# Seven block products for eight in the right half of the feed-forward down projection of a two-layer decoder trunk

## The chip, the cores and the metric

The kernel runs on one core of a Trainium2 chip. The metric is the device time of one execution in microseconds; less is better. Five engines work side by side, each through its own queue of instructions: TensorE (PE in the profile, with its weight loads as PEld), VectorE (DVE), ScalarE (ACT), GpSimd (POOL) and SyncE (SP), which here only issues DMAs. Matmul results go to PSUM, eight banks of 128 x 512 float32; everything else lives in SBUF.

## The reference

Batch 1, 256 tokens, model width 1024, two layers. Layer 0 has a dilated sliding-window attention, layer 1 a forgetting attention; each is followed by a feed-forward block with 2816 hidden features. What the change touches is the second product of that block:

```python
def swiglu(h, w_gu, w_down):
    gu = h @ w_gu
    g, u = gu[..., :D_FF], gu[..., D_FF:]
    return (jax.nn.silu(g) * u) @ w_down

def reference(x, ...):
    h = x
    for i in range(DEPTH):
        ...                                   # h = h + mixer(rmsnorm(h, ...), ...)
        h = h + swiglu(rmsnorm(h, ffn_norm[i]), ffn_w_gu[i], ffn_w_down[i])
    return rmsnorm(h, final_norm)
```

All of it is float32.

## The kernel before

**Products.** Every projection runs on TensorE in the type float32r. To keep float32 precision each operand is split into a high part (the value rounded to float32r) and a low part (what is left), and a product is three matmuls: high x high, high x low, low x high (`mm3`, L200 to L211). `mm3(o, stat, mov, ...)` loads the stationary operand, 128 columns of it, and streams the moving operand; with `narrow` the second and third matmul are cut into two halves of the columns.

**Weights.** They come in pieces of 128 x 2048 float32, two DMAs of 512 KB each into the tile `raw` (five buffers). `split` (L76) makes the high part on ScalarE (L80, `wh<-raw`) and the low part on VectorE (L84, `wl<-raw,wh`). `order` lists all pieces in the order of their use; `weights(nm, i)` returns a piece and on the way prepares the next ones, up to two ahead in the program's text. `wh` and `wl` have four buffers each.

**Order of instructions.** The kernel is written on a framework that traces it and then orders each engine's queue itself, by priority (the place in the program) and by what is ready in its own model of the time; it also draws all semaphores and gives tiles their buffers in turn. `first()` raises the priority of what stands under it by 300 instructions, `tc.issue_after` keeps an instruction behind another one.

**The feed-forward block** (`ffn`, L702, once per layer). The hidden features come in 22 blocks of 128. `up(f)` computes block f for all 256 tokens: `proj_feat` makes g, 8 products of 256 columns each (24 matmuls), ScalarE takes Silu of it (L728), a second `proj_feat` makes u, VectorE multiplies the two (L730), and `split` makes the high and low part of the result (`ah`, `al`). g goes to a PSUM bank with the tag `mm`, u to one with the tag `tr`; each tag has two banks. The first three blocks are computed token-wise and transposed instead.

Two blocks make one down piece j (11 of them per layer, NJ = 11; LATE = 8). `down(j, t)` adds, for the token half t (128 tokens), the product of the activations (stationary, 128 hidden features x 128 tokens) with the weights (moving, 512 columns) into two PSUM banks, the left 512 and the right 512 columns of the output: `acc[0]` in the banks `sc`, `acc[1]` in the banks `o`. With two halves of tokens, two blocks of hidden features and two halves of columns that is 8 products of 512 columns, 24 matmuls per piece. The sums stay in these four banks over all 11 pieces. So all eight banks are in use: `mm` and `tr` for the up projections, `sc` and `o` for the sums. Pieces alternate: after every even block f from 4 on, piece f/2 - 1 is added (piece 0 after block 3). The last pieces are taken out of order, so that the two token halves end at different times and the next stage can begin on the first; the last one in layer 1 puts its right half in two products of 256 columns in banks of their own.

Of the kernel before, what the change touches and what calls it, by code (L numbers as in the profile page):

```python
# [10 lines left out]
F32 = mybir.dt.float32  # L11
# [6 lines left out]
P = 128  # L18
# [14 lines left out]
def trunk(ctx: ExitStack, tc: tile.TileContext, T, out):  # L33
# [10 lines left out]
    def first():  # L44

        return tc.high_priority(offset=300)

    def psum(tag):
        return ps.tile([P, 512], F32, tag=tag, name=f"ps_{tag}", bufs=2)
# [26 lines left out]
    def split(pair, view, src, early=True, after=None, hold=None):  # L76
        hi, lo = pair
        with first() if early else nullcontext():
            with behind_(hold):
                a = nc.scalar.activation(view(hi), src, AF.Copy)  # L80

            def low(after=None):
                with tc.issue_after(after.ins) if after else nullcontext():
                    return nc.vector.tensor_tensor(view(lo), src, view(hi).bitcast(F32), op=ALU.subtract)  # L84

            if isinstance(after, list):
                return after.append(low)
            return a, low(after)


    def piece(key, todo=None):
        if key[0][:2] == "dn" and key[1] == LATE:
            wh, wl = (y.rearrange("p k c -> p (k c)") for y in fm_tile("ot", KT, 1))
        else:
            wh, wl = (wp.tile([P, WIDE], F32R, tag=y, name=y, bufs=4) for y in ("wh", "wl"))
        if key == GATED:
            wh, wl = (y.rearrange("p (k c) -> p k c", k=KT) for y in (wh, wl))
        for c in range(2):
            raw = wp.tile([P, 1024], F32, tag="raw", name="raw", bufs=5)
            u = slice(c * 1024, (c + 1) * 1024)  # L100
            nc.sync.dma_start(raw, T[key[0]][key[1]][:, u])
            view = lambda y, u=u: y[:, u]
            if key == GATED:
                raw = raw.rearrange("p (k c) -> p k c", c=256)
                view = lambda y, c=c: y[:, c * 4:c * 4 + 4, :256]
            cut = lambda after=None, hold=None, raw=raw, view=view: split((wh, wl), view, raw, False, after, hold)
            if todo is None:
                cut()
            else:
                todo.append(cut)  # L110
        if key == GATED:
            cut = lambda after=None, hold=None: split((wh, wl), lambda y: y[:, :, 256:], wf32, False, after, hold)
            todo.append(cut)
        return wh, wl

    def fm_tile(tag, n, bufs):
        return tuple(ap.tile([P, n, S], F32R, tag=f"{tag}{x}", name=f"{tag}{x}", bufs=bufs) for x in "hl")
# [31 lines left out]
        order += [(f"dn{l}", NJ - 1)]  # L149
    AHEAD = 2  # L150
    ready = {}
    state = {"next": 0}

    def weights(nm, i, after=None, ahead=AHEAD, hold=None):
# [56 lines left out]
    def both(pair, *idx):  # L211
        return tuple(x[idx] for x in pair)
# [84 lines left out]
    def transposed(blocks, copy=nc.vector.tensor_copy, tag="tr", home="pt"):  # L297

        tr = psum(tag)
        for i, b in enumerate(blocks):  # L300
            nc.tensor.transpose(tr[:, i * P:(i + 1) * P], b, ident)  # L301
        n = len(blocks) * P
        bufs, cols = {"pt": (3, 640), "bias": (4, 6 * P)}[home]
        w = ap.tile([P, cols], F32, tag=home, name="pt", bufs=bufs)
        with first():
            copied["last"] = copy(w[:, :n], tr[:, :n])
        return w
# [64 lines left out]
    def plus(a, b):  # L372
        return nc.vector.tensor_tensor(a, a, b, op=ALU.add)
# [328 lines left out]
    def ffn(l, hs, xt, grow, mid):  # L702
        acc = {}
        acts = {}

        def act(f):
            if f % 2 == 0:
                acts[f // 2] = tuple(p_tile(512, F32R, f"a{y}") for y in "hl")
            return acts[f // 2], lambda y: y[:, (f % 2) * S:(f % 2 + 1) * S]

        def gated(g, u, shape):
            sa = ap.tile([P, 512], F32, tag="qr", name="sa", bufs=3)
            sg, a = (sa[:, i * S:(i + 1) * S].rearrange("p (a b) -> p a b", a=shape) for i in range(2))
            nc.scalar.activation(sg, g, AF.Silu)
            nc.vector.tensor_tensor(a, u, sg, op=ALU.mult)
            return a

        def up(f):
            wt = weights(f"gu{l}", f)
            with first() if f == NF - 1 else nullcontext():  # L720
                up_with(f, wt)

        def up_with(f, wt):
            sa = ap.tile([P, 512], F32, tag="qr", name="sa", bufs=3)
            sg, a = (sa[:, i * S:(i + 1) * S] for i in range(2))
            g, u = (psum(tag)[:, :S] for tag in ("mm", "tr"))
            proj_feat(xt, wt, g, 0)
            nc.scalar.activation(sg, g, AF.Silu)  # L728
            proj_feat(xt, wt, u, 1)
            nc.vector.tensor_tensor(a, u, sg, op=ALU.mult)  # L730
            split(*act(f), a)

        def down(j, t, by_f=None, narrow=False):

            wt = dn[j]
            if j == 0:
                acc[t] = [psum(("sc", "o")[t]) for _ in range(2)]
            cols = [(0, 512, acc[t][0][:, :512]), (512, 512, acc[t][1][:, :512])]
            own = l == 1 and t == 1 and j == NJ - 1
            if own:  # L740

                acc[t][1:] = psum("mm"), psum("tr")
                cols[1:] = (512, 256, acc[t][1][:, :256]), (768, 256, acc[t][2][:, :256])
            nf = [(c, f) for c in cols for f in range(2)]
            if by_f is not None:
                nf = [(c, f) for f in by_f for c in cols]
            for (a, b, o), f in nf:
                i = mm3(o, both(acts[j], ALL, slice(f * S + t * P, f * S + (t + 1) * P)),
                        both(wt, ALL, slice(f * D + a, f * D + a + b)), f == 0 and (j == 0 or own and a >= 512),
                        f == 1 and (j == NJ - 1 or l * t * a > 0 and j == NJ - 2), narrow and (a, b, f) == (512, 512, 1))  # L750
            return i


        dn = {}
        ws = [weights(f"gu{l}", f) for f in range(2)]
        pair = [psum(("o", "mm")[l]) for _ in range(2)]
        rows = {}

        def gate(t):
            gu = pair[t].rearrange("p (a c b) -> p a c b", a=2, c=2)  # L760
            rows[t] = gated(gu[:, :, 0, :], gu[:, :, 1, :], 2)

        for half in range(2):
            proj_pair(xt, ws[half], pair, half, (0,))
        gate(0)
        wt, o = weights(f"gu{l}", 2), psum(("mm", "o")[l])
        proj_tok(xt, wt, o[:, :S], 0, hook=(2, lambda: norm_t(*hs[1], grow, xt, 1)))
        for half in range(2):
            proj_pair(xt, ws[half], pair, half, (1,))
        gate(1)  # L770
        proj_tok(xt, wt, o[:, S:], 1)
        tr = psum("tr")
        for f in range(2):
            for t in range(2):
                nc.tensor.transpose(tr[:, f * S + t * P:f * S + (t + 1) * P], rows[t][:, f, :], ident)
        act(0)
        split(acts[0], lambda y: y, tr)
        third = act(2)
        up(3)
        gu = o.rearrange("p (a c b) -> p a c b", a=2, c=2)  # L780
        a = gated(gu[:, :, 0, :], gu[:, :, 1, :], 2)
        tr = psum("tr")
        for t in range(2):
            nc.tensor.transpose(tr[:, t * P:(t + 1) * P], a[:, t, :], ident)
        split(*third, tr[:, :S])
        for f in range(2, NF):
            if f > 3:
                up(f)
            if f % 2 == 0:
                j = f // 2 - 1  # L790
                dn[j] = weights(f"dn{l}", j)
                down(j, 0, narrow=j >= LATE)
                if j < LATE:
                    down(j, 1, narrow=True)
        dn[NJ - 1] = weights(f"dn{l}", NJ - 1)
        down(LATE, 1)
        last = down(NJ - 1, 0, (0, 1))
        res = [residual(acc[0], hs[0][0], f"hf{l}0")]
        with tc.issue_after(last.ins):
            down(NJ - 2, 1)  # L800
            if l == 0:
                down(NJ - 1, 1, (0,))
            else:
                h1 = hs[1][0][:, 512:]
                with first():
                    nc.vector.tensor_tensor(h1, acc[1][1], h1, op=ALU.add)
            mid(res[0])
            down(NJ - 1, 1, (1,) if l == 0 else None)
        res.append(residual(acc[1], hs[1][0], f"hf{l}1") if l == 0 else (acc[1], hs[1][0]))
        return res  # L810
# [328 lines left out]
```

## Time and profile before

| | |
|---|---|
| median of 3 runs | 735.55 us (734.79 to 736.73) |
| the profiled execution | 736.1 us |
| its span, first to last instruction | 734.3 us |
| mean granted TensorE clock | 0.997 |
| busy: PE, PEld | 726.4 us (99%), 672.4 us (92%) |
| busy: DVE, ACT, POOL | 495.9 us (68%), 388.7 us (53%), 83.0 us (11%) |
| DMA | 141.93 MB, mean 193 GB/s |

A row of the page or of a view names line, engine and operation, then what is written and read (`out<-in`, tile names of the program without buffer numbers), the shapes, and how many. Behind a bar stand busy time and mean duration, behind a second bar the idle time of the engine just before these instructions and what ended it. In the timeline a row begins with the start in microseconds and the duration; the idle time before it stands in square brackets. TensorE's matmuls are pipelined, so their durations overlap and the distance between starts tells the pace. In a table of windows, each engine has its busy time in that stretch and in brackets the number of its instructions.

The two feed-forward blocks run from about 253 to 436 us and from about 545 us to the end. One period of their middle part, two up projections and one down piece, takes 16.4 us.

### The profile page before, as it was taken

Reading aid. Unit: us, or ns where it says so; the run is one execution under the profiler, and the core shown is the slowest. Engines: PE = TensorE matmul, PEld = TensorE weight load, DVE = VectorE, ACT = ScalarE, POOL = GpSimd, SP = SyncE. Lnnn points to the kernel's source line nnn. Section 1 sums busy time; section 2 is a strip of 40 time slices with the busy share of each in tenths; the row PEclk is TensorE's granted clock in tenths of the full one; section 3 lists DMA queues with packets and bytes.
Section 4 is the critical chain, followed back from the end, with each engine's and each line's share of the span. In section 5 each row is a group of like instructions: output and inputs, shape, how many; then the busy total and the mean of one; then the engine's idle time right before and its main releaser. Section 6 shows DMA issues by size and latency. Waiting matters only on the chain.

```text
span 734.3 us, 14310 instructions
## 1 busy us (share of the span) xinstructions
PE 726.4 (99%) x5856; PEld 672.4 (92%) x5856; DVE 495.9 (68%) x762; ACT 388.7 (53%) x617; POOL 83.0 (11%) x118
## 2 busy tenths in 40 slices
PE   9999999999999999999999999999999999999996
PEld 7999989999988899999999989999889999999995
DVE  6997998998996775554555474576776554556533
ACT  7646747738445663444554453587475444545421
POOL 0600206007105000000000004110010000000001
PEclk9999999999999999999999999999999999999998
DMA  9865955956864376656567352874547656656601
GB/s 335 306 202 174 237 182 153 289 193 152 268 194 160 116 241 221 195 179 203 195 202 247 127 168 90 294 260 138 172 142 237 222 179 203 195 188 218 198 1 58
DMA packets 55042, 141.93 MB, mean 193 GB/s; under 512 B 20257, under 2 KB 21441, under 8 KB 54977
## 3 DMA queue, kind: packets, MB, share of 16 engines
q1 hardware_dynamic: 54832, 140.88, 59.4%
q8 instruction: 46, 0.75, 0.4%
q14 instruction: 20, 0.16, 0.1%
q10 hardware_dynamic: 144, 0.15, 0.1%
HBM read 136.00 MB, written 1.07 MB: 187 GB/s over the span
## 4 chain that ended last, share of the span: by engine, by line
PE 97%; DVE 1%; ACT 1%; POOL 0%; issue 0%; POOLq 0%; DVEq 0%; ACTq 0%
PE ps_mm L208 34%; PE ps_mm L203 17%; PE ps_tr L208 9%; PE ps_sc L208 8%; PE ps_o L208 7%; PE ps_tr L203 5%; PE ps_sc L203 4%; PE ps_o L203 4%; PE ps_o L313 2%; PE ps_sc L395 2%; PE ps_tr L196 1%; PE ps_tr L301 1%; PE ps_sc L476 1%; PE ps_o L322 1%; PE ps_sc L894 0%; PE ps_sc L458 0%
## 5 line engine op out<-in xcount | busy, mean ns | idle before, releaser
L80 ACT ACTIVATE wh<-raw 128x1024 fp32r<-128x1024 f32 x236 | 243.4, 1054 | 207.1 <-PE ps_tr L208 66.7
L84 DVE TENSOR_TENSOR wl<-raw,wh 128x1024 fp32r<-128x1024 f32 x236 | 288.3, 1242 | 82.6 <-ACT wh L80 82.4
L203 PE MATMUL ps_mm<-xt,wh 128*128 128x256 f32 x816 | 227.2, 279 | 0.2 <-ACT v L281 0.2
L208 PE MATMUL ps_mm<-xt,wl 128*128 128x256 f32 x816 | 226.0, 277 | 0.0
L208 PE MATMUL ps_mm<-xt,wh 128*128 128x256 f32 x816 | 226.0, 277 | 0.0
L203 PEld LDWEIGHTS ps_mm<-xt,wh 128*128 128x128 f32 x816 | 153.1, 188 | 2.2 <-issue 1.7
L208 PEld LDWEIGHTS ps_mm<-xt,wl 128*128 128x128 f32 x816 | 153.6, 188 | 0.1
L208 PEld LDWEIGHTS ps_mm<-xt,wh 128*128 128x128 f32 x816 | 153.4, 188 | 0.0
L208 PE MATMUL ps_tr<-xt,wh 128*128 128x256 f32 x304 | 83.9, 276 | 0.0
L208 PE MATMUL ps_tr<-xt,wl 128*128 128x256 f32 x304 | 83.9, 276 | 0.0
L203 PE MATMUL ps_tr<-xt,wh 128*128 128x256 f32 x304 | 83.7, 276 | 0.0
L730 DVE TENSOR_TENSOR sa<-ps_tr,sa 128x256 f32<-128x256 f32 x38 | 16.1, 424 | 73.5 <-PE ps_tr L208 73.5
L208 PEld LDWEIGHTS ps_tr<-xt,wh 128*128 128x128 f32 x304 | 57.1, 188 | 0.0
L208 PEld LDWEIGHTS ps_tr<-xt,wl 128*128 128x128 f32 x304 | 57.0, 188 | 0.0
L203 PEld LDWEIGHTS ps_tr<-xt,wh 128*128 128x128 f32 x304 | 57.0, 188 | 0.0
L203 PE MATMUL ps_mm<-wh,xt 128*128 128x512 f32 (+1 forms) x144 | 49.8, 346 | 0.0
L173 POOL TENSOR_SCALAR rs<-ssq 128x1 f32<-128x1 f32 x7 | 1.9, 271 | 420.6 <-ACT junk L182 420.6
L208 PE MATMUL ps_mm<-wl,xt 128*128 128x512 f32 (+1 forms) x149 | 49.1, 335 | 0.0
L208 PE MATMUL ps_mm<-wh,xt 128*128 128x512 f32 (+1 forms) x149 | 49.1, 335 | 0.0
L285 POOL COPY v<-v 32x256 f32<-32x256 f32 x64 | 40.5, 632 | 71.2 <-ACT v L281 68.6
L203 PE MATMUL ps_sc<-wh,ah 128*128 128x512 f32 x80 | 31.4, 392 | 0.0
L208 PE MATMUL ps_sc<-wl,ah 128*128 128x512 f32 (+1 forms) x82 | 31.3, 385 | 0.0
(232 smaller groups left out, 1113.6 us busy)
## 6 DMA issues: line engine op xcount, KB each, us to landing
raw<-in_gu SPq DMA_DIRECT2D x88, 512.0 KB, 4.8
raw<-in_a_in SPq DMA_DIRECT2D x68, 512.0 KB, 5.0
raw<-in_dn SPq DMA_DIRECT2D x44, 512.0 KB, 4.7
raw<-in_b_in SPq DMA_DIRECT2D x24, 512.0 KB, 5.0
raw<-in_a_out SPq DMA_DIRECT2D x8, 512.0 KB, 5.0
raw<-in_b_out SPq DMA_DIRECT2D x8, 512.0 KB, 4.4
bias<-sums SPq DMA_DIRECT2D x8, 384.0 KB, 6.6
grow<-in_norms SPq DMA_DIRECT2D x4, 512.0 KB, 5.7
```

Source lines behind the costliest of these rows:

```text
L80: a = nc.scalar.activation(view(hi), src, AF.Copy)
L84: return nc.vector.tensor_tensor(view(lo), src, view(hi).bitcast(F32), op=ALU.subtract)
L196: nc.tensor.transpose(tr[:, k * P:(k + 1) * P], xn[:, kk * P:(kk + 1) * P], ident)
L203: nc.tensor.matmul(o, sh, mh, start=start, stop=False)
L208: last = nc.tensor.matmul(o[:, u], s, m[:, u], start=False, stop=end and u.stop == n)
L285: nc.gpsimd.tensor_copy(v[1 + a % 2][n:n + 32, a // 2 * S:a // 2 * S + S], by_t[a * 32:a * 32 + 32, t, g])
L301: nc.tensor.transpose(tr[:, i * P:(i + 1) * P], b, ident)
L313: nc.tensor.matmul(o[h * HD:(h + 1) * HD], v[:, c:c + HD], w(h), start=start, stop=stop)
L322: nc.tensor.matmul(o[:, :n], mhalf.to_broadcast([P, P]), mhalf.to_broadcast([P, n]), start=True, stop=True)
L395: nc.tensor.matmul(lead[t], xt[y][:, k, t * P:(t + 1) * P], w[z][:, u], start=k + y + z == 0, stop=k == KT - 1 and z == 1)
L476: nc.tensor.matmul(sc[h][c, o:o + 64], q[HR[h], pr, qb * P + a * 32:qb * P + a * 32 + 32], k[HR[h], pr].rearrange("p (b n) -> p b n", b=2) ...
L730: nc.vector.tensor_tensor(a, u, sg, op=ALU.mult)
```

## The change

In pieces 0 to 7 of each layer, the right half of the output is computed by Strassen's scheme in Winograd's form. For one piece the right half is a product of two 2 x 2 matrices of blocks: two token halves x two blocks of hidden features, times two blocks of hidden features x two column groups of 256. Eight block products become seven, with sums of blocks made beforehand on both sides and sums of products afterwards.

- `sums_of` takes the place of the loop in `piece` for these weights. From the four 128 x 256 blocks it makes four sums on VectorE; one overwrites a block of `raw`, three go to a tile of 768 columns (`ts`, tag `pt`) that is split like a weight (`th`, `tl`, tag `bias`).
- `combine` makes four sums of activation blocks with three instructions on VectorE (`sa4`, tag `pt`) and splits them (`sh`, `sl`, tag `v`). For this the unsplit activations of a pair of blocks are kept together (`pair_of`, tag `qr`); for the first three blocks ScalarE copies them from PSUM.
- `down` computes only the left columns in these pieces, without `narrow`; `down_7` adds the seven products of 256 columns into seven areas of 256 columns: three in the right banks of `acc`, four in two more banks, `acc["x"]`.
- `acc["x"]` takes the two `tr` banks from piece 0 to piece 7. So in every `up` after the first blocks, g and u share one bank with the tag `mm`, g in columns 0 to 255, u in columns 256 to 511.
- `gather`, after piece 7, adds the products that belong to several output blocks to the residual rows h (a copy on ScalarE, eight additions on VectorE) and so frees the `tr` banks.
- The first product of the right half that follows for the second token half (piece 8) is done in two groups of 256 columns, as half of that bank has not been written before.

```diff
@@ piece
+        if key[0][:2] == "dn" and key[1] < LATE:
+            todo += sums_of(key, (wh, wl))
+            return wh, wl
         for c in range(2):
...
+    def sums_of(key, w):
+
+        raw = [wp.tile([P, 1024], F32, tag="raw", name="raw", bufs=5) for _ in range(2)]
+        for c in range(2):
+            nc.sync.dma_start(raw[c], T[key[0]][key[1]][:, c * 1024:(c + 1) * 1024])
+        b11, b12, b21, b22 = (raw[f][:, c:c + S] for f in range(2) for c in (512, 768))
+        sums = ap.tile([P, 768], F32, tag="pt", name="ts", bufs=3)
+        t3, t2, t4 = (sums[:, i * S:(i + 1) * S] for i in range(3))
+        pair = tuple(ap.tile([P, 768], F32R, tag="bias", name=f"t{y}", bufs=4) for y in "hl")
+        summed[key] = pair
+
+        def plus(o, a, b):
+            nc.vector.tensor_tensor(o, a, b, op=ALU.add)
+
+        def cut(c, after=None, hold=None):
+            if c == 0:
+                plus(t3, b12, b22)
+                plus(b12, b11, b12)
+            elif c == 2:
+                plus(t2, b22, b12)
+                plus(t4, t2, b21)
+                return split(pair, lambda y: y, sums, False, after, hold)
+            return split(w, lambda y: y[:, c * 1024:(c + 1) * 1024], raw[c], False, after, hold)
+
+        return [lambda after=None, hold=None, c=c: cut(c, after, hold) for c in range(3)]
@@ ffn
+        rows_f = {}
+        combos = {}
+
+        def pair_of(j):
+            if j not in rows_f:
+                rows_f[j] = ap.tile([P, 512], F32, tag="qr", name="a2", bufs=3)
+            return rows_f[j]
+
+        def combine(j, a):
+
+            y = ap.tile([P, 512], F32, tag="pt", name="sa4", bufs=3)
+            b = a.rearrange("p (b c) -> p b c", c=P)
+            z = y.rearrange("p (b c) -> p b c", c=P)
+            with first():
+                nc.vector.tensor_tensor(z[:, :2], b[:, 1:2].to_broadcast([P, 2, P]), b[:, 0:4:3], op=ALU.subtract)
+                nc.vector.tensor_tensor(z[:, 2], z[:, 1], b[:, 0], op=ALU.subtract)
+                nc.vector.tensor_tensor(z[:, 3], b[:, 2], z[:, 2], op=ALU.add)
+            combos[j] = tuple(ap.tile([P, 512], F32R, tag="v", name=f"s{x}", bufs=7) for x in "hl")
+            split(combos[j], lambda y: y, y)
+
+        def down_7(j):
+
+            if j == 0:
+                acc["x"] = [psum("tr") for _ in range(2)]
+            c11, c12, c21, _, p1, p6, q5, q7 = (x[:, i * S:(i + 1) * S]
+                                                for x in (acc[0][1], acc[1][1], *acc["x"]) for i in range(2))
+            a, w, s, t = acts[j], dn[j], combos[j], summed[f"dn{l}", j]
+            for o, (st, i), (mv, c) in ((p1, (a, 0), (w, 512)), (c11, (a, 2), (w, D + 512)), (c12, (s, 3), (w, D + 768)),
+                                        (c21, (a, 3), (t, 512)), (q5, (s, 1), (w, 768)), (p6, (s, 2), (t, S)),
+                                        (q7, (s, 0), (t, 0))):
+                mm3(o, both(st, ALL, slice(i * P, (i + 1) * P)), both(mv, ALL, slice(c, c + S)),
+                    j == 0 and any(o is y for y in (p1, c11, c21, q5)), j == LATE - 1 and any(o is y for y in (p6, q7)))
+
+        def gather():
+
+            (p1, p6), (q5, q7) = ((x[:, :S], x[:, S:]) for x in acc["x"])
+            y = ap.tile([P, 512], F32, tag="pt", name="u", bufs=3)
+            u, d = y[:, :S], y[:, S:]
+            h0, h1 = hs[0][0], hs[1][0]
+            c0, c1 = slice(512, 768), slice(768, 1024)
+            nc.scalar.activation(d, p1, AF.Copy)
+            for o, x, z, op in ((u, d, p6, ALU.add), (h0[:, c0], h0[:, c0], d, ALU.add), (d, q5, u, ALU.subtract),
...
@@ up_with
-            sa = ap.tile([P, 512], F32, tag="qr", name="sa", bufs=3)
-            sg, a = (sa[:, i * S:(i + 1) * S] for i in range(2))
-            g, u = (psum(tag)[:, :S] for tag in ("mm", "tr"))
+            sg = ap.tile([P, 512], F32, tag="qr", name="sa", bufs=3)[:, :S]
+            a = pair_of(f // 2)[:, f % 2 * S:(f % 2 + 1) * S]
+            o = psum("mm")
+            g, u = o[:, :S], o[:, S:]
             proj_feat(xt, wt, g, 0)
             nc.scalar.activation(sg, g, AF.Silu)
             proj_feat(xt, wt, u, 1)
             nc.vector.tensor_tensor(a, u, sg, op=ALU.mult)
             split(*act(f), a)
+            if f % 2 and 1 < f // 2 < LATE:
+                combine(f // 2, rows_f.pop(f // 2))
@@ down
-            cols = [(0, 512, acc[t][0][:, :512]), (512, 512, acc[t][1][:, :512])]
+            cols = [(0, 512, acc[t][0][:, :512])]
+            if j >= LATE:
+                cols.append((512, 512, acc[t][1][:, :512]))
...
+                if (j, t, a, f) == (LATE, 1, 512, 0):
+
+                    st = both(acts[j], ALL, slice(P, 2 * P))
+                    for c in (0, S):
+                        mm3(o[:, c:c + S], st, both(wt, ALL, slice(a + c, a + c + S)), False, False)
+                    continue
@@ the loop of ffn
                 down(j, 0, narrow=j >= LATE)
                 if j < LATE:
-                    down(j, 1, narrow=True)
+                    down(j, 1)
+                    down_7(j)
+                if j == LATE - 1:
+                    gather()
```

The tag `pt` grows from 640 to 768 columns. For the first three blocks the same activations are also copied (`pair_of(0)`, `rows_f[1]`) and combined.

More of the change, by code (lines that the diff above doesn't have):

```diff
@@ L151, in trunk @@
     ready = {}
+    summed = {}
     state = {"next": 0}
@@ L302, in transposed @@
         n = len(blocks) * P
-        bufs, cols = {"pt": (3, 640), "bias": (4, 6 * P)}[home]
+        bufs, cols = {"pt": (3, 768), "bias": (4, 6 * P)}[home]
         w = ap.tile([P, cols], F32, tag=home, name="pt", bufs=bufs)
@@ new lines, in gather @@
+        def gather():
[6 more added lines that the diff above has]
+            for o, x, z, op in ((u, d, p6, ALU.add), (h0[:, c0], h0[:, c0], d, ALU.add), (d, q5, u, ALU.subtract),
+                                (h0[:, c1], h0[:, c1], d, ALU.add), (h1[:, c1], h1[:, c1], d, ALU.add),
+                                (h1[:, c1], q7, h1[:, c1], ALU.add), (h1[:, c0], h1[:, c0], u, ALU.add),
+                                (h1[:, c0], h1[:, c0], q7, ALU.subtract)):
+                nc.vector.tensor_tensor(o, x, z, op=op)
@@ L777, in ffn @@
         split(acts[0], lambda y: y, tr)
+        nc.scalar.activation(pair_of(0), tr, AF.Copy)
+        combine(0, rows_f.pop(0))
         third = act(2)
@@ L785, in ffn @@
         split(*third, tr[:, :S])
+        nc.scalar.activation(rows_f[1][:, :S], tr[:, :S], AF.Copy)
+        combine(1, rows_f.pop(1))
         for f in range(2, NF):
```

## The prediction

> **What bounds the kernel now.** I read the page first: engines, then the chain that ended last, then who waited for whom.
>
> ```profile
> span 734.3 us, 14310 instructions
> PE 726.4 (99%) x5856; PEld 672.4 (92%) x5856; DVE 495.9 (68%) x762; ACT 388.7 (53%) x617; POOL 83.0 (11%) x118
> ...
> PE 97%; DVE 1%; ACT 1%; POOL 0%; issue 0%; POOLq 0%; DVEq 0%; ACTq 0%
> ```
>
> TensorE (PE) is the chain. The list of PE's own waits has two lines for the whole kernel:
>
> ```profile
> PE ps_o L322 <- DVE mhalf L66: 0.9, 1, 0.9
> PE ps_mm L203 <- ACT v L281: 0.2, 1, 0.2
> ```
>
> So time is won only by giving PE fewer columns to stream, and lost as soon as PE has to wait. What a column costs is read from start to start in the timeline of PE (the durations overlap). One down piece, and the ends of the up projection (one feature block) around it:
>
> ```profile
> 299.19 0.28 PE L203 MATMUL ps_mm<-xt,wh 128*128 128x256 f32 x1
> ...
> 301.80 0.28 PE L208 MATMUL ps_mm<-xt,wl 128*128 128x256 f32 x1
> 301.91 0.28 PE L203 MATMUL ps_tr<-xt,wh 128*128 128x256 f32 x1
> ...
> 304.63 0.39 PE L203 MATMUL ps_sc<-wh,ah 128*128 128x512 f32 x1
> 304.87 0.40 PE L208 MATMUL ps_sc<-wl,ah 128*128 128x512 f32 x1
> 305.10 0.39 PE L208 MATMUL ps_sc<-wh,al 128*128 128x512 f32 x1
> 305.33 0.39 PE L203 MATMUL ps_sc<-wh,ah 128*128 128x512 f32 x1
> 305.56 0.39 PE L208 MATMUL ps_sc<-wl,ah 128*128 128x512 f32 x1
> ...
> 307.37 0.39 PE L203 MATMUL ps_o<-wh,ah 128*128 128x512 f32 x1
> ...
> 309.64 0.40 PE L208 MATMUL ps_o<-wl,ah 128*128 128x256 f32 x2
> 309.87 0.40 PE L208 MATMUL ps_o<-wh,al 128*128 128x256 f32 x2
> 310.11 0.29 PE L203 MATMUL ps_mm<-xt,wh 128*128 128x256 f32 x1
> 310.23 0.28 PE L208 MATMUL ps_mm<-xt,wh 128*128 128x256 f32 x1
> ```
>
> An up projection is 48 matmuls of 256 columns, 299.19 to 304.63: 0.1133 us each. The piece lasts 310.11 - 304.63 = 5.48 us. It has 24 products of 512 columns; the last two are cut into 2 x 256. In steady state a 512 takes 0.227 us (307.37 to 309.64 is 10 of them), but the first three after 256-wide work take 0.24, 0.23, 0.23.
>
> **The change part by part, PE first.** Per piece the left halves keep 12 products of 512: 307.37 - 304.63 = 2.74 us. The right half loses 12 products of 512 (5.48 - 2.74 = 2.74 us) and gets 7 blocks x 3 = 21 products of 256. These have activations as the stationary operand and weights moving, so the nearest row is the only place before where such products stand in a row, the last twelve of the kernel:
>
> ```profile
> 725.91 0.28 PE L203 MATMUL ps_mm<-wh,ah 128*128 128x256 f32 x1
> 726.03 0.28 PE L208 MATMUL ps_mm<-wl,ah 128*128 128x256 f32 x1
> ...
> 727.23 0.28 PE L208 MATMUL ps_tr<-wh,al 128*128 128x256 f32 x1
> ```
>
> Eleven steps in 1.32 us: 0.120 each, not the 0.1133 of the up projections. Bounds of the new block: 21 x 0.1133 = 2.38 and 21 x 0.120 = 2.52 us. I take 0.120, the row with the same roles. A piece then takes 2.74 + 2.52 = 5.26, 0.22 us less; eight pieces in two layers give 16 x 0.22 = 3.5 us. With 0.1133 it is 0.36 a piece, 5.8 us; that is the best the change can do.
>
> Nine more weight loads per piece (21 for 12) cost nothing extra beyond this, as loads run beside matmuls:
>
> ```profile
> 410.07 0.28 PE L203 MATMUL ps_tr<-xt,wh 128*128 128x256 f32 x1
> 410.07 0.19 PEld L208 LDWEIGHTS ps_tr<-xt,wh 128*128 128x128 f32 x1
> ```
>
> A load of 0.19 us starts with a matmul, and the next matmul follows after 0.11. Without that cover nine loads at 0.19 would add 1.7 us a piece, 27 us in all. [...]
>
> In the first late piece (index 8) one product of 512 is now two groups of 256: six at 0.120 for three at 0.227, +0.04 us, twice: +0.1.
>
> **The moved bank, the part that can turn the sign.** The "tr" PSUM buffers now hold Strassen sums from the first to the eighth down piece, so gate g and up u of a block share one "mm" bank. ScalarE reads g (Silu) while PE used to start u at once in another bank. Does one engine wait for another in the same bank though the columns differ? Before shows one such place: the gate columns 256 to 271 of a bank are read on VectorE (L945), columns 0 to 255 on ScalarE (L946).
>
> ```profile
> L946 ACT ACTIVATE v<-ps_sc x2: 367/376/385, 440.7 to 450.2; 128x256 f32<-128x256 f32 x2
> its engine sat idle before it (us, times) until:
>   DVE gates L945: 0.4, 1
> ```
>
> L946 needs nothing from L945, yet it waits. So u's first matmul will wait for Silu of g. [...] The price if PE just stands there:
>
> ```profile
> 302.11 0.39 ACT L728 ACTIVATE sa<-ps_mm 128x256 f32<-128x256 f32 x1 [0.46 <-PE ps_mm L208]
> 304.77 1.06 ACT L80 ACTIVATE wh<-raw 128x1024 fp32r<-128x1024 f32 x1 [2.27 <-PE ps_tr L208]
> ```
>
> Silu ends at 302.50; u could begin then and not at 301.91: 0.59 us. L728 ran 38 times: 22 us. That is one end; the other is nothing, if other matmuls stand between g and u. The scheduler of the framework, which orders each engine's queue, does not keep to program order. Before, the program has g and u of block 20, then of block 21; PE ran:
>
> ```profile
> 411.00:416.50 5.50, 5.41 (x48) 5.49 (x48) 0.00 (x0) 0.00 (x0) 1.00 0.31 100
> 416.50:422.00 5.50, 5.47 (x48) 5.43 (x48) 0.42 (x1) 0.00 (x0) 1.00 0.28 95
> ```
>
> (windows; first row the ps_mm instructions, second the ps_tr ones): both g first, then both u. Block 21 has raised priority there, but it shows that a matmul that can go is put ahead of one that can't. Independent work is always at hand: after an odd block the next block's g (its bank was freed one up projection earlier), after an even one the left half of a down piece. Six matmuls of 256 or three of 512 cover 0.59 us. I take the low end, filled, with a remainder between 0 and about 0.1 us where the scheduler's idea of Silu is short. The fill costs two more changes of width per even block: 0.24 + 0.23 + 0.23 against 3 x 0.227 at the start of 512 is +0.02, and 0.12 against 0.1133 for the first 256s after it (310.11 to 310.23) +0.02; 9 blocks x 2 layers x 0.04 = 0.7 us.
>
> **VectorE and ScalarE, off the path.** One period (two up projections and a piece):
>
> ```profile
> 304.60:321.00 16.40, 16.40 (x124) 15.53 (x123) 8.61 (x10) 7.42 (x10) 0.00 (x0) 1.00 0.60 194
> L84 DVE TENSOR_TENSOR wl<-raw,wh 128x1024 fp32r<-128x1024 f32 x6 | 7.2, 1222 | 4.0 <-ACT wh L80 4.0
> L80 ACT ACTIVATE wh<-raw 128x1024 fp32r<-128x1024 f32 x6 | 6.2, 1054 | 7.8 <-PE ps_tr L208 4.5 <-issue 3.3
> L84 DVE TENSOR_TENSOR al<-sa,ah 128x256 fp32r<-128x256 f32 x2 | 0.8, 418 | 0.0
> L80 ACT ACTIVATE ah<-sa 128x256 fp32r<-128x256 f32 x2 | 0.8, 402 | 0.0
> ```
>
> Between 256 and 1024 columns VectorE goes by 1.05 ns a column, ScalarE by 0.85. Added on VectorE per piece: four weight sums of 256 (1.68), the low part of 768 columns (0.95), activation sums of 256, 128, 128 (0.42 + 0.28 + 0.28) and a low part of 512 (0.69): 4.3 us; on ScalarE the high parts of 768 and 512: 0.84 + 0.62 = 1.5. So 12.9 and 8.9 us of a period of 16.1: 80% and 55%. Neither becomes the bound. I cost it at nothing because weights are split far ahead: the wh row at 304.77 waits for PE (a buffer freed at the end of an up projection, four in rotation), not for data, so a split starts some three pieces, 16 us, before it is used, and 4.3 us later is still early. If that cover went, PE would wait for wl: up to 4.3 us a piece, 69 us. No DMA is added. SyncE issues the same two loads per piece; their raw buffers are freed later by the four sums, delaying the loads behind them by as much, under the same cover.
>
> Two PSUM reads by ScalarE (about 0.6 and 0.4 us) and the first sums come early in each layer, 2.7 us or more before the first block product; gather (a copy and eight additions, about 3.8 us) touches h, which is read three pieces later. Nothing for both.
>
> **Sum.** 3.5 - 0.1 - 0.7 = 2.7 us. The profiled execution took 736.1 us (span 734.3 and 1.8 around it): 733.4. It stood 0.5 us above the median of the three runs, 735.55, which gives 732.8, 0.4% less. About 0.3%, 2.2 us, is what a measurement of this kernel can tell from no change.
>
> **Rivals.**
> First, the forecast: filled, products at 0.113 to 0.120, 2 to 5.8 us won: 729.8 to 733.5. Chance 0.56, of which 0.04 falls within 0.3%.
> Second, filled but short: the fill is planned, Silu comes later on the chip (behind a 1.05 us split on ScalarE, say) and a remainder stays at each of the 38 hand-offs. At 0.07 us it eats the 2.7 us; at 0.13 us the kernel is 0.3% slower; at 0.2 us it gives 740.5. For it: ScalarE gets busier. Against: PE's wait list shows no such misjudged hand-off. Chance 0.25, 0.17 of it within 0.3%, 0.03 faster, 0.05 slower.
> Third, the other sign: no fill, PE stands from g's end until Silu's end, 38 x 0.59 = 22 us less the 3.4 won: 754. The L946 row speaks for the wait, the 48/48 windows against standing still. Decided from 0.13 us per hand-off. Chance 0.11.
> Fourth, the sums come too late for PE, at the start of a layer where splits compete most, or the saving is lost otherwise: 735 to 740. Chance 0.06, 0.02 of it within 0.3%.
> Fifth, exposed weight loads: nine at 0.19 us per piece, 27 us less 3.5 won: 759. The load row speaks against. Chance 0.02.
> Together: faster 0.52 + 0.03 = 0.55, within 0.3% 0.04 + 0.17 + 0.02 = 0.23, slower 0.22. The range for 8 in 10 runs from the best case, 729.8, to 740; the likeliest case alone holds 729.8 to 733.5.
>
> **What would show it.** On PE, 21 matmuls of 256 after the left halves, spaced 0.113 to 0.120, piece about 5.1 to 5.3 us. Between the last matmul of g and the first of u in one bank, matmuls of another tile (ps_mm of the next block, ps_sc of a piece); if there are none, the third rival. PE's wait list: lines "PE ps_mm <- ACT sa" are the second or third rival, "<- DVE wl" or a wait for the new sums the fourth. VectorE about 565 us busy (495.9 + 16 x 4.3), ScalarE about 413, PE still the chain. The forecast is wrong if those waits sum to more than 2.7 us.

## The result, and the profile after

The changed kernel takes 761.66 us (median, 759.54 to 765.1) against 735.17 us for the kernel before (four runs, 734.78 to 736.73; the first three had the median 735.55): a ratio of 1.0361, 95% interval 1.0319 to 1.0402. The forecast was 732.8 us, faster. The profiled execution took 759.54 us, its span is 757.7 us, 23.4 us longer than before.

The page of the changed kernel, its first lines and its chain:

```profile
span 757.7 us, 14722 instructions
PE 736.5 (97%) x5974; PEld 678.6 (90%) x5974; DVE 563.1 (74%) x922; ACT 411.8 (54%) x655; POOL 83.8 (11%) x118
...
PE 73%; DVE 9%; DMA 9%; ACT 5%; issue 3%; POOL 0%; POOLq 0%; DVEq 0%; ACTq 0%; SPq 0%
```

Before, the chain was PE for 97% of the span. Now it leaves PE for a quarter of it. PE's 97% is no proof that it is full, as its durations overlap (0.28 us for a matmul of 256 columns, the next one started after 0.11 to 0.12); of the others VectorE is busiest, with 74%. So the time went into waits. The list of PE's own waits gives the place (total, times, longest):

```profile
PE ps_mm L233 <- ACT sa L805: 11.2, 9, 2.8
```

L233 is the first matmul of a product in `mm3`, L805 is Silu. PE waits for Silu before it writes the up product u in the bank that still holds the gate product g. The list names only nine of the places. The others show in the timeline as steps between starts that are too long. First the end of g of an odd block, PE's rows and then ScalarE's:

```profile
318.31 0.28 PE L238 MATMUL ps_mm<-xt,wl 128*128 128x256 f32 x1
318.42 0.74 PE L233 MATMUL ps_mm<-xt,wh 128*128 128x256 f32 x2
319.00 0.28 PE L238 MATMUL ps_mm<-xt,wh 128*128 128x256 f32 x1
```

```profile
318.34 0.38 ACT L805 ACTIVATE sa<-ps_mm 128x256 f32<-128x256 f32 x1 [1.44 <-PE ps_mm L238]
```

The row with x2 holds two matmuls of L233, at 318.42 and 318.78 by the trace. The first is one matmul of the next block's g, the whole fill; the second opens u, 0.06 us after Silu's end at 318.72. The step is 0.36 us in place of 0.113, and the next one, to 319.00, is 0.22. This hand-off costs about 0.37 us, where 0.36 - 0.11 is the wait and the rest a slow restart. After an even block there is more fill, and it is still too short, because Silu is not the next thing in ScalarE's queue (PE, then ScalarE):

```profile
323.89 0.39 PE L233 MATMUL ps_sc<-wh,ah 128*128 128x512 f32 x1
...
324.59 0.39 PE L233 MATMUL ps_sc<-wh,ah 128*128 128x512 f32 x1
324.88 0.39 PE L233 MATMUL ps_mm<-xt,wh 128*128 128x256 f32 x1
325.10 0.28 PE L238 MATMUL ps_mm<-xt,wh 128*128 128x256 f32 x1
```

```profile
322.98 1.05 ACT L80 ACTIVATE wh<-raw 128x1024 fp32r<-128x1024 f32 x1
323.93 0.61 ACT L80 ACTIVATE sh<-sa 128x512 fp32r<-128x512 f32 x1
324.46 0.37 ACT L805 ACTIVATE sa<-ps_mm 128x256 f32<-128x256 f32 x1
```

Four matmuls of 512 columns stand between g and u, 0.9 us, but Silu sits behind a weight split and the split of the activation sums and starts only at 324.46. The step to u is 0.29 us in place of the 0.23 of a 512 and the next one again 0.22, so PE is short by about 0.2 us here. The worst place is where that queue itself waits for a load or a sum (ScalarE, then PE):

```profile
293.37 1.06 ACT L80 ACTIVATE wh<-raw 128x1024 fp32r<-128x1024 f32 x1 [4.68 <-DMA raw<-in_dn]
294.34 0.40 ACT L80 ACTIVATE ah<-a 128x256 fp32r<-128x256 f32 x1
294.64 2.94 ACT L80 ACTIVATE wh<-raw 128x1024 fp32r<-128x1024 f32 x3
299.00 0.84 ACT L80 ACTIVATE th<-ts 128x768 fp32r<-128x768 f32 x1 [1.42 <-DVE ts L131]
299.75 0.37 ACT L805 ACTIVATE sa<-ps_mm 128x256 f32<-128x256 f32 x1
```

```profile
297.09 0.28 PE L233 MATMUL ps_mm<-xt,wh 128*128 128x256 f32 x1
300.17 0.38 PE L233 MATMUL ps_mm<-xt,wh 128*128 128x256 f32 x1 [2.80 <-ACT sa L805]
```

ScalarE stands idle 4.7 us for a load and 1.4 us for sums, and Silu stands behind both in its queue: PE, which has run g, loses 3 us. That such waits cost PE little by themselves is shown below, by the run with the added load alone. Six places like this one, where ScalarE waits for a load, a sum or a combination of activations ahead of Silu or has several splits ahead of it, hold 11 of the 18.7 us of stalls in the table below.

All steps between matmul starts in the two feed-forward blocks (252 to 436 us and from 545 us on), less 0.4427 ns a column (the 5.44 us for 48 matmuls of 256 columns in the kernel before), add up like this:

| excess, us (steps) | before | after |
|---|---|---|
| stalls | 0.3 (4) | 18.7 (38) |
| first steps after a stall, about 0.22 us | none | 3.6 (33) |
| steps of about 0.21 us, half pace | 0.35 (4) | 4.0 (40) |
| all other steps | 3.5 | 7.2 |

The sum grows by 29.3 us. The columns saved are 16 pieces x 768 x 0.4427 ns = 5.4 us. The difference, 23.9 us, is close to the 23.4 us between the spans.

### The profile page after: what moved, and what is told of

Its sections match the earlier page's. It is cut to its first block, busy times and chain, and to the rows that moved or that the text cites. A ratio compares the mean times of both kernels' runs of the same rounds, so it can differ in the third digit from the quotient of the medians.

```text
span 757.7 us, 14722 instructions
## 1 busy us (share of the span) xinstructions
PE 736.5 (97%) x5974; PEld 678.6 (90%) x5974; DVE 563.1 (74%) x922; ACT 411.8 (54%) x655; POOL 83.8 (11%) x118
## 4 chain that ended last, share of the span: by engine, by line
PE 73%; DVE 9%; DMA 9%; ACT 5%; issue 3%; POOL 0%; POOLq 0%; DVEq 0%; ACTq 0%; SPq 0%
PE ps_mm L238 32%; PE ps_mm L233 17%; DMA raw<-in_dn 8%; PE ps_sc L238 6%; PE ps_o L238 4%; DVE wl L84 4%; ACT wh L80 4%; PE ps_sc L233 3%; PE ps_o L233 2%; PE ps_o L343 2%; PE ps_sc L425 2%; ACT sa L805 1%; PE ps_tr L238 1%; DMA raw<-in_gu 1%; PE ps_tr L226 1%
## 5 line engine op out<-in xcount | busy, mean ns | idle before, releaser
L233 PE MATMUL ps_mm<-xt,wh 128*128 128x256 f32 x1120 | 317.2, 283 | 13.4 <-ACT sa L805 11.2
L238 PE MATMUL ps_mm<-xt,wh 128*128 128x256 f32 x1120 | 311.0, 278 | 0.0
L238 PE MATMUL ps_mm<-xt,wl 128*128 128x256 f32 x1120 | 310.9, 278 | 0.0
L233 PEld LDWEIGHTS ps_mm<-xt,wh 128*128 128x128 f32 x1120 | 211.9, 189 | 26.3 <-ACT sa L805 23.2
L238 PEld LDWEIGHTS ps_mm<-xt,wl 128*128 128x128 f32 x1120 | 212.2, 189 | 0.0
L238 PEld LDWEIGHTS ps_mm<-xt,wh 128*128 128x128 f32 x1120 | 212.0, 189 | 0.1
L807 DVE TENSOR_TENSOR a<-ps_mm,sa 128x256 f32<-128x256 f32 x38 | 16.1, 424 | 68.0 <-PE ps_mm L238 67.8
L233 PE MATMUL ps_mm<-wh,xt 128*128 128x512 f32 (+1 forms) x144 | 49.8, 346 | 0.0
L238 PEld LDWEIGHTS ps_mm<-wl,xt 128*128 128x128 f32 x149 | 28.0, 188 | 3.1
L238 PEld LDWEIGHTS ps_mm<-wh,xt 128*128 128x128 f32 x149 | 27.6, 188 | 3.1
L233 PEld LDWEIGHTS ps_mm<-wh,xt 128*128 128x128 f32 x144 | 27.0, 188 | 3.6 <-issue 0.3
L805 ACT ACTIVATE sa<-ps_mm 128x256 f32<-128x256 f32 x38 | 14.1, 375 | 28.6 <-PE ps_mm L238 28.4
L561 ACT COPY pt<-turned 128x1280 uint16<-128x1280 uint16 x12 | 19.5, 1668 | 13.2 <-DMA turned<-pt 13.2
L558 POOL COPY pt<-p 128x1280 uint16<-128x1280 uint16 x12 | 17.5, 1477 | 77.5 <-DVE p L538 37.9
L238 PE MATMUL ps_sc<-wh,al 128*128 128x512 f32 (+1 forms) x66 | 23.6, 363 | 0.1
```

Of the source, the lines that this page charges most:

```text
L233: nc.tensor.matmul(o, sh, mh, start=start, stop=False)
L238: last = nc.tensor.matmul(o[:, u], s, m[:, u], start=False, stop=end and u.stop == n)
L558: nc.gpsimd.tensor_copy(split16.rearrange("p (t c) -> p t c", t=2), parts(quad["pt"][pr, h]))
L561: nc.scalar.copy(parts(w), turned.rearrange("p (t c) -> p t c", t=2))
```

## The experiments

The theory: g and u in one bank make PE wait for ScalarE at each block, since the fill is short or missing (the hand-off). The rival: the added sums, splits and later loads are themselves too late for PE (the load).

**Own banks again.** The change, with a `mm` bank each for g and u:

```diff
-            o = psum("mm")
-            g, u = o[:, :S], o[:, S:]
+            g, u = (psum("mm")[:, :S] for _ in range(2))
```

> The changed kernel, but g and u of a block take one mm bank each again (the two mm banks in turn, one for g and one for u); products, sums and the two tr banks for Strassen sums stay. Hand-off theory (u waits in PE's queue for Silu of g, because they share a bank, and so for whatever stands before Silu in ScalarE's queue): all of the loss goes, 731 to 734 us, about 16 x 0.22 us under before. Load theory (VectorE's 4.3 us more per piece makes weights or activations late for PE, whatever the banks): most of the loss stays, over 748 us, and PE's wait list names wl, al or the sums.

Measured 744.35 us, ratio 1.0118 (1.0095 to 1.0142). Some 17 of the 26 us are gone. Neither theory's range was met: all of the loss was expected to go, and 8 us stay. In PE's waits the hand-off has moved: the next g uses its one bank again and waits for Silu there.

```profile
PE ps_mm L233 <- ACT sa L804: 6.4, 4, 3.1
```

The longest of these four, ScalarE's rows and then PE's: a late load of piece 8 (the tile `oth`, which PE first reads 24 us later) stands ahead of Silu.

```profile
384.09 1.06 ACT L80 ACTIVATE oth<-raw 128x1024 fp32r<-128x1024 f32 x1 [3.96 <-DMA raw<-in_dn]
385.05 0.37 ACT L804 ACTIVATE sa<-ps_mm 128x256 f32<-128x256 f32 x1
```

```profile
385.47 0.58 PE L233 MATMUL ps_mm<-xt,wh 128*128 128x256 f32 x1 [3.11 <-ACT sa L804]
```

**The bank alone.** The kernel before, all products and splits as they were, g and u in halves of one `mm` bank (the edit above the other way round).

> The kernel before with the shared bank alone: g and u in the two halves of one mm bank, the tr banks idle, no Strassen products and no sums. Hand-off theory: 38 hand-offs at the 0.35 us that the quiet ones of the changed kernel show, 745 to 750 us, with all gaps on PE between g (or its fill) and u. Load theory: the hand-offs are mostly filled, and the time is 735 to 738 us.

Measured 752.18 us, ratio 1.0213 (1.0195 to 1.0231). The shared bank by itself, with none of the added work, costs 16 us over 38 blocks, a little more than the 745 to 750 us expected. That is 0.42 us a block as a mean, not at each: the quiet waits cost about 0.3 us each, one in two blocks, and two waits of 1.6 and 1.8 us, with a stretch at half pace behind the second (granted clock 0.53), hold over 6 us. Even here a late load is passed on; ScalarE's rows at the split of piece 8:

```profile
383.18 1.06 ACT L80 ACTIVATE oth<-raw 128x1024 fp32r<-128x1024 f32 x1 [1.73 <-DMA raw<-in_dn]
384.14 0.37 ACT L729 ACTIVATE sa<-ps_mm 128x256 f32<-128x256 f32 x1
```

**The load alone.** The added sums and splits of the change, unused, with the products and the four banks of the kernel before:

```diff
-                plus(b12, b11, b12)
+                plus(t2, b11, b12)
...
-            o = psum("mm")
-            g, u = o[:, :S], o[:, S:]
+            g, u = (psum(tag)[:, :S] for tag in ("mm", "tr"))
...
-            cols = [(0, 512, acc[t][0][:, :512])]
-            if j >= LATE:
-                cols.append((512, 512, acc[t][1][:, :512]))
+            cols = [(0, 512, acc[t][0][:, :512]), (512, 512, acc[t][1][:, :512])]
...
-                    down(j, 1)
-                    down_7(j)
-                if j == LATE - 1:
-                    gather()
+                    down(j, 1, narrow=True)
```

> The kernel before (eight products, g and u in mm and tr) with all sums of weights and activations and their splits done as in the changed kernel, and not used; gather is left out. Hand-off theory: 735 to 736 us, as PE waits for none of it. Load theory: 745 us or more.

Measured 736.76 us, ratio 1.0013 (1.0001 to 1.0024), with VectorE busy 554.6 us. That is 0.7 us above before, just over the 735 to 736 us expected. With four banks the load is hidden but for less than 1 us. PE's wait list has one new entry, at the start of the first feed-forward; it comes up again below:

```profile
PE ps_tr L864 <- DVE sa L791: 0.9, 1, 0.9
```

The rival is out as a cause on its own.

**No sums.** The change without its additions on either side; the splits read the unsummed blocks.

```diff
-                plus(t3, b12, b22)
-                plus(b12, b11, b12)
+                pass
...
-                plus(t2, b22, b12)
-                plus(t4, t2, b21)
-                return split(pair, lambda y: y, sums, False, after, hold)
+                return split(pair, lambda y: y, raw[1][:, :768], False, after, hold)
...
-            split(combos[j], lambda y: y, y)
+            split(combos[j], lambda y: y, a)
```

> The changed kernel with its shared bank and seven products, but without the seven additions per piece on VectorE: the sums' splits take unsummed blocks instead (values are not the reference's). VectorE loses about 2.6 us a piece. Hand-off theory: the quiet part of the loss stays (38 x 0.35 us less 3.5 to 5.4), 743 to 750 us, and the hand-offs of over 1 us go or shrink, as raw buffers come free earlier and ScalarE's queue is not held up before Silu. Load theory: 731 to 736 us.

Measured 763.75 us, ratio 1.0363 (1.0338 to 1.0389): nothing gained, and the expected 743 to 750 us was wrong. Taking VectorE's additions away does not free Silu. Of ScalarE's waits from 252 to 436 us, first in the change, then here:

```profile
ACT th L80 <- DVE ts L131: 20.2, 7, 3.2
```

```profile
ACT th L80 <- DMA raw<-in_dn: 21.4, 7, 4.6
```

Without the sums the same split waits as long for the load. The reading that fits is that any instruction with late data ahead of Silu in the queue does the harm, whoever makes the data. One thing differs besides: the split of the right half now reads the tile `raw` itself and holds it longer, which can delay the loads behind it; this run doesn't tell the two apart.

**Two banks before.** The kernel before with a bank each for g and u, two in place of four in turn (the first edit, on the kernel before), to see what the 8 us of the first experiment are.

> The kernel before with one edit: gate and up products get two banks of their own, used by every block, in place of four in turn; products, splits and sums as before. It asks what the 8 us are that the change with two banks (744.35 us) still loses. Theory A (the work): the added splits and late loads stand ahead of Silu in ScalarE's queue and pass on only because g's bank is used again at once; without them two banks cost little: 735 to 738 us. Theory B (the banks): one bank for g costs a hand-off at every block whatever the rest does: 741 to 746 us.

Measured 737.19 us, ratio 1.0023 (1.0013 to 1.0032): the work theory held. Two banks cost 1.6 us with the old work, the load 0.7 us with four banks; both together, with the block products, 8. The rows of the first experiment show where they meet: in ScalarE's queue, where a late split stands ahead of Silu.

**Ordered fill.** The change, with TensorE's work between g and u fixed. For an even block `fill` is `down(j, 0)` and `down(j, 1)`, for an odd one `down_7(j)`:

```diff
-            proj_feat(xt, wt, g, 0)
+            last = proj_feat(xt, wt, g, 0)
             nc.scalar.activation(sg, g, AF.Silu)
-            proj_feat(xt, wt, u, 1)
+            if fill:
+                with tc.issue_after(last.ins):
+                    last = fill()
+            with tc.issue_after(last.ins) if fill else nullcontext():
+                proj_feat(xt, wt, u, 1)
```

> The whole change with its shared bank, one thing ordered: TensorE's work between a block's gate product and its up product is no longer left to the scheduler. After the gate product of an even block come the two left-half products of the piece (12 matmuls of 512 columns, about 2.7 us), after that of an odd block the seven block products (21 of 256 columns, about 2.5 us), and only then the up product; blocks 19 and 21 stay unfilled. Theory A (the hand-off, fill too short): Silu has read the bank before the up product starts, the 18.7 us of stalls shrink to 1 to 3 us with the restarts and slow stretches behind them, and the time is 731 to 737 us, perhaps under the kernel before. Theory B (sums and loads late): the splits of sums and loads are still late, the stalls move to the down products or stay, 748 to 760 us.

Measured 742.24 us, ratio 1.0088 (1.0072 to 1.0104). It takes back 19 of 26 us; PE's waits for Silu shrink from 11.2 us to this:

```profile
PE ps_mm L233 <- ACT sa L807: 1.9, 3, 1.1
PE ps_sc L238 <- DVE al L84: 1.4, 3, 0.5
```

The expected 731 to 737 us was missed, and the rival's 748 to 760 too: 6.6 us of stalls remain, about half of them still in front of a u, the others where PE needs `al` or another split part; they are taken up below.

**Ordered fill, two banks.** The same with the first edit.

> The ordered fill as in the run before, and a bank each for gate and up product in place of halves of one. Theory A: with 2.5 us of other products between, the next gate product finds Silu done just as the up product does; within 1 us of the run with the shared bank, 731 to 737 us. Theory B (sharing a bank costs by itself, beyond the wait for Silu): faster than the shared bank by 2 us or more.

Measured 740.71 us, ratio 1.0062 (1.0045 to 1.0079). That is 1.5 us faster than with the shared bank, between the less than 1 us of theory A and the 2 us or more of B, and above the 731 to 737 us expected. The intervals overlap: once there is enough work between, sharing costs some 1.5 us more or nothing, which stays open.

**Silu elsewhere.** The change, with Silu reading a tile in SBUF.

```diff
-            nc.scalar.activation(sg, g, AF.Silu)
+            nc.scalar.activation(sg, grow[:, :S], AF.Silu)
```

> The whole change, but Silu of blocks 3 to 21 reads 256 columns of a tile in SBUF in place of the gate product; the values differ by that, all else is issued as in the change. The up product then waits for no read of its bank. Theory A (Silu's read of the shared bank, the hand-off): nearly all of the 26 us goes, 733 to 739 us. Theory B (sums and loads are late for the products themselves): above 748 us.

Measured 737.25 us, ratio 1.0026 (1.0008 to 1.0043). With Silu's read of the shared bank taken away, 24.4 of the 26.5 us go. More than the read goes with it, though: Silu no longer waits for g, the framework puts it far ahead (the last one starts at 706.5 us, in the change at 731.8), and so nothing that is late in ScalarE's queue reaches PE through it. The run prices the whole hand-off, the bank and what stands ahead of Silu together. It also says what this version is worth with the hand-off gone: still 1.6 us slower than before, not 2.7 faster. About half of its 6.7 us of stalls sits at the start of the two feed-forwards; the first, PE and then VectorE:

```profile
276.43 0.39 PE L238 MATMUL ps_sc<-wl,ah 128*128 128x512 f32 x1
278.99 0.41 PE L873 MATMUL ps_tr<-ident,sa 128*128 128x128 f32 x2 [2.18 <-DVE sa L791]
```

```profile
275.71 0.43 DVE L749 TENSOR_TENSOR sa<-a 128x256 f32<-128x256 f32 x1 [0.67 <-ACT a L865]
276.17 0.29 DVE L750 TENSOR_TENSOR sa<-sa,a 128x128 f32<-128x128 f32 x1
276.50 0.29 DVE L751 TENSOR_TENSOR sa<-a,sa 128x128 f32<-128x128 f32 x1
...
278.43 0.41 DVE L791 TENSOR_TENSOR sa<-ps_mm,sa 128x256 f32<-128x256 f32 x1
```

The sums for piece 0 (L749 to L751) have raised priority; the product of the third block (L791), which PE's transposes wait for, comes after them. The other half is mostly waits of up to 0.8 us in the middle, where PE needs the parts `al`, `ah` or `sl` of activations or of their sums.

**Fill, with a narrow end.** The ordered fill, with the last left-half product's second and third matmul cut into columns of 256 (`down(j, 1, narrow=True)`, and the condition in `down` made to hold for a = 0).

> The ordered fill (742.24 us), and the last left-half product of each piece issued as columns of 256 in place of 512. In the ordered fill the 48 matmuls of 256 columns that follow the 512-column products run at 0.118 us each all the way, while behind 256-column products they are back at 0.1135 us after three. Theory A (the pace after 512-column matmuls stays slow until a run of 256s settles it): the 48 settle, 16 times 48 times 4.4 ns less 16 times about 0.05 us, so 2 to 3 us faster, 739 to 741 us. Theory B (the slow pace belongs to these weights or to the load on the memory): same time as the ordered fill, 741.5 to 743 us.

Measured 742.17 us, ratio 1.0086 (1.0066 to 1.0107): the time of theory B. The pace does what theory A expected. The first matmul of the 48 and the first one behind them, in the ordered fill and then here:

```profile
338.17 0.28 PE L233 MATMUL ps_mm<-xt,wh 128*128 128x256 f32 x1
...
343.82 0.28 PE L233 MATMUL ps_tr<-wh,ah 128*128 128x256 f32 x1
```

```profile
336.34 0.29 PE L233 MATMUL ps_mm<-xt,wh 128*128 128x256 f32 x1
...
341.80 0.28 PE L233 MATMUL ps_tr<-wh,ah 128*128 128x256 f32 x1
```

5.65 us against 5.46, 0.118 and 0.114 each. The profiled span fell from 740.6 to 738.4 us, the median did not; the stalls of this profile are larger, 7.7 against 6.6 us. Whether the 2 us come through in the mean stays open.

**Six pieces.** As the run before, with eight products in pieces 0 and 1 too; among the edits:

```diff
+    FIRST = 2
-        if key[0][:2] == "dn" and key[1] < LATE:
+        if key[0][:2] == "dn" and FIRST <= key[1] < LATE:
...
-            if j >= LATE:
+            if not FIRST <= j < LATE:
...
-        nc.scalar.activation(pair_of(0), tr, AF.Copy)
-        combine(0, rows_f.pop(0))
```

> As the run before, with seven block products only in the pieces 2 to 7; pieces 0 and 1, at the start of a feed-forward, use eight, as in the kernel before, so their copies, combinations and sums of blocks (on VectorE and ScalarE just where the first gates are multiplied) go. Theory A (the early sums are late): the stalls of 1.4 us at 274 us and 2.6 us at 569 and 591 us go, and 4 pieces at 0.2 to 0.3 us of gain are given up: 735 to 738.5 us. Theory B (those stalls are there from loads or from the gating itself): 739 to 742 us.

Measured 739.19 us, ratio 1.0038 (1.0026 to 1.005), a little above the 735 to 738.5 expected and just inside the rival's 739 to 742. In the profile it is theory A: the stalls at the start of the feed-forwards are gone (4.5 us of stalls left in all), and the run is 3.0 us faster than the one before, although a quarter of the block products was given up. What stays is at block 18; PE, then ScalarE:

```profile
383.64 0.40 PE L239 MATMUL ps_sc<-wh,al 128*128 128x512 f32 x1
384.57 0.50 PE L234 MATMUL ps_sc<-wh,ah 128*128 128x512 f32 x1 [0.53 <-ACT ah L80]
```

```profile
381.25 1.06 ACT L80 ACTIVATE oth<-raw 128x1024 fp32r<-128x1024 f32 x1 [2.04 <-DMA raw<-in_dn]
382.22 1.99 ACT L80 ACTIVATE wh<-raw 128x1024 fp32r<-128x1024 f32 x2
384.12 0.40 ACT L80 ACTIVATE ah<-a 128x256 fp32r<-128x256 f32 x1
```

Again a late load in ScalarE's queue; this time the activations' high part stands behind it.

**Sums on GpSimd.** As the run before, the four weight sums on GpSimd.

```diff
-            nc.vector.tensor_tensor(o, a, b, op=ALU.add)
+            nc.gpsimd.tensor_tensor(o, a, b, op=ALU.add)
```

> As the run before, with the four sums of weight blocks per piece on GpSimd in place of VectorE, so that neither they nor the loads they wait for stand ahead of VectorE's low parts and gate products. Theory A (late low parts stand behind the sums on VectorE): the last stalls of about 1 us at 385 and 681 us go, 1 to 2.5 us faster than six pieces with sums on VectorE, near 734 to 736 us. Theory B (GpSimd is slower at these sums than the 0.4 us of VectorE, and the high parts of the sums on ScalarE wait for them): same or slower, 737 to 745 us.

Measured 744.51 us, ratio 1.0128 (1.0102 to 1.0154): theory B. GpSimd takes 0.72 to 1.76 us for a sum that took VectorE 0.42, the split waits for it, and Silu for the split:

```profile
283.95 1.76 POOL L131 TENSOR_TENSOR ts<-raw 128x256 f32<-128x256 f32 x1 [25.81 <-DMA raw<-in_dn]
...
288.28 0.72 POOL L131 TENSOR_TENSOR ts<-ts,raw 128x256 f32<-128x256 f32 x1
```

```profile
289.04 0.84 ACT L80 ACTIVATE th<-ts 128x768 fp32r<-128x768 f32 x1 [4.23 <-POOL ts L131]
289.78 0.37 ACT L808 ACTIVATE sa<-ps_mm 128x256 f32<-128x256 f32 x1
```

No version that ran is faster than the kernel before.

## Why the prediction was wrong

**The step that failed is the moved bank.** The prediction saw that u would wait for Silu, and priced an unfilled hand-off at 0.59 us, 22 us in all. It then took "the low end, filled, with a remainder between 0 and about 0.1 us". It measured 0.64 us as a mean (761.66 against 737.25 us, 24.4 us over 38), of which six long waits are a large part. Two arguments behind "filled" did not hold. A matmul that can go is not always put ahead: after an odd block the whole fill was one matmul of 0.113 us, the first of the next g, and the rest of that g came behind u. Why the framework stopped there is not shown. And six matmuls of 256 or three of 512 do not cover Silu's delay: four of 512 were there after the even block shown and were too few, since Silu waits behind splits of 1.05 and 0.61 us. The absence of misjudged hand-offs in PE's waits before was no evidence either: with four banks in turn no Silu was urgent, so none could show there. The prediction's own sign of being wrong, waits of more than 2.7 us in PE's list, came out at 11.2 us. That u waits for Silu at all was forecast rightly. The wait is a semaphore that the framework sets; what the chip would do without it no run here tries.

**The rivals.** The third (no fill, 754 us) came nearest in time, the second (filled but short, Silu behind a split) names the mechanism of the even blocks. Both conditions occurred in turn, the third's but for one matmul, and what neither held is the third part: a load or a sum that is late in ScalarE's queue stops Silu and with it PE, up to 3 us at a time. The shared bank alone gives a mean of 0.42 us a block; the remaining 0.22 appears only together with the change's own work.

**The products** were right. One piece's 21, first start to the start behind them:

```profile
291.52 0.28 PE L233 MATMUL ps_tr<-wh,ah 128*128 128x256 f32 x1
...
294.02 0.28 PE L233 MATMUL ps_mm<-xt,wh 128*128 128x256 f32 x1
```

2.50 us, 0.119 each; predicted 2.52 at 0.120. The weight loads stayed hidden: 0.19 us each in the trace, one to every step of 0.119. So the fifth rival is out.

**VectorE and ScalarE** were right in size (563.1 and 411.8 us busy; predicted 565 and 413). "At nothing" nearly holds with four banks (0.7 us in the load-alone run). It does not hold once Silu is urgent: the cover named was that of the weights, and the queue that carries the splits is also the one that carries Silu.

**The early copies and sums,** "nothing for both", cost more: the 2.2 us wait for L791 at 276 us with Silu out of the way, and one of 0.4 us at the start of the second feed-forward, 3.3 us of stalls with the steps around them. No such stall is left in the run where pieces 0 and 1 use eight products. With the waits for split parts in the middle that makes 6.7 us of stalls against 0.3 before, enough for the 4.4 us between the 737.25 us without the hand-off and the 732.8 forecast. The fourth rival (late sums at the start of a layer) had the early sums, at a chance of 0.06; they are a cause of their own, as the same wait with four banks shows, but a small one beside the hand-off.

**The width changes** were put at 0.7 us for the even blocks, with 0.02 us a time for the first 256s behind the 512s. In the ordered fill the slow pace did not end with the first ones: the 48 matmuls shown above took 5.65 us where 48 x 0.1133 is 5.44, 4.4 ns more each, 0.21 us for one up projection.

## What to carry to other kernels

When a change takes buffers away, ask what those buffers kept from being urgent: here two banks kept PE from ever needing Silu, and a queue in which loads could be late at no cost became part of PE's path. A hand-off between engines should be priced by what stands in the other engine's queue ahead of it, and by the fill that is fixed in the order, not by fill that is merely available. A saving of 5.4 us of columns, 0.7% of the time, in many small products needs its extra work off every queue that the bound engine waits for.

## What the runs showed of the hardware

After some long waits TensorE restarts at half pace. Windows of the changed kernel (us, PE busy, PEclk, DMA share, GB/s):

```profile
297.10:300.10 3.00, 0.27 (x3) 1.00 0.45 130
300.20:303.70 3.50, 3.50 (x17) 0.54 0.86 274
303.80:306.80 3.00, 3.00 (x27) 0.98 0.57 231
```

For 3.5 us after the wait the granted clock is 0.54, and 256 columns take 0.213 us. In the changed kernel steps of 3.08 and 2.81 us between matmul starts were followed by such a stretch (granted clock 0.54 and 0.58), steps of 2.26 and 2.08 us were not (1.00 behind both). The length alone does not decide it: with the shared bank alone a step of 2.08 us was followed by it (first two rows), and with Silu elsewhere one of 2.56 us was not (third row, the stretch behind it):

```profile
681.90:683.90 2.00, 0.27 (x3) 1.00 0.63 197
684.00:687.50 3.50, 3.50 (x17) 0.53 0.78 276
```

```profile
279.00:282.50 3.50, 3.50 (x23) 1.00 0.00 0
```

Ahead of these stretches PE stood idle for 1.8 us in the run with the shared bank alone and for 2.8 us in the changed kernel; with Silu elsewhere it stood idle for 2.18 us and went on at a granted clock of 1.00. What decides between waits of like length, no run here shows.

After the other waits the first step of 256 columns takes 0.22 us and the next three 0.113 to 0.123, some 0.13 us more than four steps of 0.1133 (the 33 such first steps hold 3.6 us in the table above).

In the ordered fill 48 matmuls of 256 columns behind 512-column ones took 5.65 us, 0.118 each; with the narrow end, behind 256-column ones, the 48 took 5.46 us, 0.114 each.
